# A decoder trunk on one core: the last norm on VectorE alone, modulation matmuls in quarters to four output rows, state-space parameters through GpSimd's queue, and the Toeplitz block shifted by TensorE

## The chip, the core and the metric

One core of a Trainium2 chip runs the whole kernel as one program. The metric is the time of one execution on the device in microseconds (us), as the median of several runs. The core's engines are TensorE (PE; its weight loads stand as PEld), VectorE (DVE), ScalarE (ACT), GpSimd (POOL) and SyncE (SP), which only issues transfers. Transfers can be issued by SyncE's queue and by GpSimd's.

## The reference, cut to what matters

```python
c_act = jax.nn.silu(c)
mod = c_act @ w_ada + b_ada                       # 6 vectors of 1024
sh1, sc1, g1, sh2, sc2, g2 = split(mod, 6)
h = rmsnorm(x, norm1_gain) * (1 + sc1) + sh1      # x: 1024 x 1024
proj = h @ w_in                                   # columns of four head groups
o_sb = stick_breaking_attention(...)              # 4 heads of 64, blocks of 128
o_sw = sliding_window_attention(..., rel_bias, sinks)
o_fx = forgetting_attention(...)
o_ssm = s5_ssm(u, lam, log_dt, b, c, d_skip, w_glu, b_glu)   # 16 groups of 16 channels
x = x + g1 * (groupnorm(concat(o_sb, o_sw, o_fx, o_ssm)) @ w_out)
h = rmsnorm(x, norm2_gain) * (1 + sc2) + sh2
x = x + g2 * (square(relu(h @ w_mlp_in)) @ w_mlp_out)         # 1024 -> 4096 -> 1024
return rmsnorm(x, final_gain)
```

All of it is in 32-bit floats. The large products keep that precision by splitting each operand into a high and a low part and summing three matmuls.

## The kernel before, in words

The program `tile_trunk` is written as one long sequence; a planner of the framework fixes, when the program is built, the order of the instructions on every engine, from estimates of their lengths and dependences. So an edit at one place can move instructions elsewhere on the same engine. Tiles of a pool with one tag share a fixed number of buffers.

The stages, by the trace of the kernel before:

- 0 to 57 us: x and the shift and scale quarters of `w_ada` are loaded. `shift_scale` (L210) multiplies the activated condition, widened to 32 columns, with them (L217), four matmuls of 128 columns per weight tile, to the output rows 0, 32, 64 and 96 upwards. `norm` scales the rows; `modulate` (L196) makes, for each of eight column blocks and two halves of the rows, a block of h with shift and scale in 32 bits (L199, VectorE), its rounded high part from the same source (L200, ScalarE) and the low part as the difference (L201; VectorE, for odd blocks of the second half GpSimd).
- 57 to 120 us: the projections of the stick-breaking heads (`mm3`, L253 to L255); beside them `ssm_prep` (L347) with many small VectorE instructions. There `cmul` makes complex products of six instructions each (L441 to L446): the powers `er`, `ei` and the products `qr`, `qi` on GpSimd. The parameters of the state-space head are loaded by SyncE (L331 to L340). The convolution block `kt` of 128 x 256 is written to device memory (`TD`) in eight copies shifted by 16 rows each, with zeros above (L541 and the line behind it). `window_bias` (L555) makes the bias of the sliding window.
- 115 to 350 us: stick-breaking attention by `sb_row`: scores (L639, L653), log-sigmoid and exponent on ScalarE, the mask product, the scan and the weighting on VectorE (L660, L662, L665), exponent (L666), transposes (L700) and mixing (L705). In between the other projections run, and `ada_rest` (L293), a generator that a row of attention advances three steps at a time: a step loads a weight tile of 128 x 1024 for one of four modulation vectors (L303) and multiplies it with the activated condition (L307).
- 350 to 600 us: `ssm_main`, forgetting and sliding-window attention (L733), out-projection.
- 600 to 664 us: the second norm and modulation by the same `modulate`, for `half0` and its fellows.
- 664 to 950 and 955 to 1262 us: the two products of the MLP.
- the end: `finish(t)` (L1378) for each of eight row tiles, after the tile's last sums: squares on ScalarE (L1385), a root by an estimate and one correction step (`rsqrt_mean`, L83 to L92), and the scaling by root and gain. Odd tiles (`FD_DVE`) do that with one VectorE instruction per half (L1390), even ones with ScalarE (L1393) and GpSimd (L1394).

Of the kernel before, what the change touches and what calls it, by code (L numbers as in the profile page):

```python
# [33 lines left out]
def tile_trunk(ctx: ExitStack, tc: tile.TileContext, a: dict, out: bass.AP):  # L34
# [69 lines left out]
    FD_DVE, EL = (1, 3, 5, 7), 2  # L104
# [142 lines left out]
    for f in range(KT):  # L247
        modulate(early, turn(ps1, "z", x1, f), f, h1s, h1b, hT[1][0][:, f], hT[1][1][:, f], G if f % 2 else V)
# [100 lines left out]
    def ssm_prep(pp):  # L349
# [130 lines left out]
        SY.dma_start(out=ED[0], in_=er)  # L480
        SY.dma_start(out=ED[1], in_=ei)
# [11 lines left out]
        cmul(qr, qi, pw(pr, 0), pw(pi, 0), mh(bbr), mh(bbi), sp4(d1), sp4(d2), G)  # L493
# [20 lines left out]
        SY.dma_start(out=WD[0], in_=wr.rearrange("p t k h -> p t (k h)"))  # L514
        SY.dma_start(out=WD[1], in_=wi.rearrange("p t k h -> p t (k h)"))
# [18 lines left out]
        z2 = pp.tile([P, 256], F32, name="z2")  # L534
        V.memset(z2, 0.0)
        for i in range(8):
            n = 16 * (7 - i)
            gh = lambda y: y.rearrange("q (g h) -> q g h", h=16)
            SY.dma_start(out=TD[n:P, :, i, :], in_=gh(kt[0:P - n, :]))
            if n:  # L540
                SY.dma_start(out=TD[0:n, :, i, :], in_=gh(z2[0:n, :]))  # L541
        for r, q in enumerate((qr, qi)):
            for b in range(2):
                ps = psm.tile([P, 4, P], F32, tag="ss", name="ps")
                for t in range(4):
# [3 lines left out]
                SY.dma_start(out=VTD[r][:, 4 * b:4 * b + 4, :], in_=vt)  # L549
# [6 lines left out]
    def window_bias(pp):  # L556
# [9 lines left out]
        SY.dma_start(out=RD, in_=rr[0:4, 0:384])  # L566
# [5 lines left out]
        SY.dma_start(out=Bf.rearrange("p (h c) -> p h c", h=4),  # L572
# [805 lines left out]
    def finish(t):  # L1378

        y = acc[t]  # L1380
        ss = sx.tile([P, 2], F32, tag="n3ss", bufs=2, name="ss")
        halves = [slice(n * 512, n * 512 + 512) for n in range(2)]
        for n, cs in enumerate(halves):
            sq = sx.tile([P, 512], F32, tag="sq", bufs=2, name="sq")
            A.activation(sq, y[:, cs], AF.Square, accum_out=ss[:, n:n + 1])  # L1385
        V.tensor_tensor(ss[:, 0:1], ss[:, 0:1], ss[:, 1:2], op=ALU.add)
        r = rsqrt_mean(sx, ss[:, 0:1], D, 1, "n3")
        for n, cs in enumerate(halves):
            if t in FD_DVE:
                V.scalar_tensor_tensor(out=y[:, cs], in0=y[:, cs], scalar=r[:, 0:1], in1=fg[:, cs],  # L1390
                                       op0=ALU.mult, op1=ALU.mult)
            else:
                A.activation(y[:, cs], y[:, cs], AF.Copy, scale=r[:, 0:1])  # L1393
                G.tensor_tensor(y[:, cs], y[:, cs], fg[:, cs], op=ALU.mult)  # L1394
            SY.dma_start(out=out[t * P:(t + 1) * P, cs], in_=y[:, cs])
# [95 lines left out]
```

## Time and profile before

| what | value |
|---|---|
| runs | 1277.53, 1278.24, 1279.88 us, median 1278.24 |
| the profiled execution, whole time | 1281.41 us |
| its span in the trace | 1279.3 us |
| mean granted TensorE clock | 0.976 of full speed |
| moved by transfers | 205.37 MB, 161 GB/s on average |

The span runs from the first to the last instruction of the trace; the profiled execution's own time is 2.1 us longer, and it is 3.2 us longer than the median of the runs. The page lists how long every engine was busy; windows show the same for a stretch of the span, with the clock that TensorE was granted in it (1.00 is 2.4 GHz, 0.5 is 1.2 GHz) and the share of the transfer engines. Waits and the chain name what ended an engine's idle time.

### The profile page before, as it was taken

The numbers are of one execution on the slowest core, as the hardware profiler recorded it, in microseconds if no ns is written. First come the engines' busy times: TensorE is split into PE (matmuls) and PEld (weight loads), VectorE is DVE, ScalarE is ACT, GpSimd is POOL, SyncE is SP. The second block draws the span as 40 slices with busy tenths as digits, with TensorE's granted clock in tenths as the row PEclk, the third lists the DMA queues.
The fourth block names the chain that finished last, engine by engine and source line by source line (L and its number), as shares of the span: only waits on it lengthen the run. The fifth ranks groups of instructions, "written<-read, shape, count | busy, mean of one in ns | idle before, by whom it ended". The sixth has DMA issues, their size and how long they took to land.

```text
span 1279.3 us, 18741 instructions
## 1 busy us (share of the span) xinstructions
PE 1214.4 (95%) x6461; PEld 945.6 (74%) x6461; DVE 955.3 (75%) x2100; ACT 562.4 (44%) x1205; POOL 125.3 (10%) x171
## 2 busy tenths in 40 slices
PE   5899899999999998999899999999989999999994
PEld 3578677665677776888668888888867888888883
DVE  4685977775465687888998677767666777788998
ACT  4433555762224557545563232333344543433425
POOL 1218100000020100000000000000031210100003
PEclk9999899999999898999989999999999999999997
DMA  8664376576654655202124553443578653643413
GB/s 297 201 198 146 139 195 212 175 221 185 215 175 153 238 152 175 88 26 83 67 66 166 172 167 131 155 154 130 170 250 315 213 168 108 182 127 91 138 48 132
DMA packets 139334, 205.37 MB, mean 161 GB/s; under 512 B 37057, under 2 KB 77912, under 8 KB 139240
## 3 DMA queue, kind: packets, MB, share of 16 engines
q1 hardware_dynamic: 129768, 170.62, 41.6%
q0 software_dynamic: 9472, 33.56, 8.4%
q8 instruction: 51, 0.84, 0.3%
q14 instruction: 43, 0.35, 0.1%
HBM read 144.59 MB, written 59.55 MB: 160 GB/s over the span
## 4 chain that ended last, share of the span: by engine, by line
PE 80%; DVE 8%; DMA 7%; ACT 2%; issue 2%; SPq 1%; DVEq 0%; ACTq 0%
PE x L255 9%; PE x L253 9%; PE x L254 8%; PE y L254 6%; PE y L255 6%; PE y L253 6%; PE ps L253 6%; PE ps L254 6%; PE ps L255 6%; PE pv L705 3%; PE tp L700 3%; PE z L639 3%; PE ps L307 2%; DMA wa<-in_w_ada_dram 2%; DMA kk<-kd 1%
## 5 line engine op out<-in xcount | busy, mean ns | idle before, releaser
L1091 ACT CAST hi<-s 128x512 fp32r<-128x512 f32 x124 | 75.9, 618 | 110.8 <-PE x L254 36.7
L1091 ACT CAST hi<-hid 128x512 fp32r<-128x512 f32 x101 | 62.2, 618 | 129.7 <-issue 58.1
L254 PE MATMUL x<-lo,hi 128*128 128x512 f32 x256 | 98.3, 389 | 0.3 <-DVE lo L1092 0.3
L253 PE MATMUL x<-hi 128*128 128x512 f32 x256 | 95.9, 390 | 2.4 <-ACT hi L1091 2.4
L255 PE MATMUL x<-hi,lo 128*128 128x512 f32 x256 | 97.8, 389 | 0.0
L1092 DVE TENSOR_TENSOR lo<-raw,hi 128x512 fp32r<-128x512 f32 x97 | 65.9, 686 | 40.8 <-PE x L255 21.6
L253 PE MATMUL ps<-hT_hi,wh 128*128 128x512 f32 x224 | 90.8, 417 | 4.9 <-DVE e L273 2.6
L255 PE MATMUL ps<-hT_hi,wl 128*128 128x512 f32 x224 | 91.5, 411 | 1.5 <-DVE wl L185 1.5
L1091 ACT CAST hi<-raw 128x512 fp32r<-128x512 f32 x97 | 59.1, 619 | 74.2 <-PE y L254 45.9
L254 PE MATMUL ps<-hT_lo,wh 128*128 128x512 f32 x224 | 91.2, 408 | 0.0
L1092 DVE TENSOR_TENSOR lo<-s,hi 128x512 fp32r<-128x512 f32 x124 | 84.2, 684 | 3.1 <-ACT hi L1091 2.1
L1092 DVE TENSOR_TENSOR lo<-hid,hi 128x512 fp32r<-128x512 f32 x101 | 69.1, 685 | 21.1 <-ACT hi L1091 19.0
L255 PE MATMUL y<-hi,lo 128*128 128x512 f32 x196 | 75.3, 389 | 0.0
L254 PE MATMUL y<-lo,hi 128*128 128x512 f32 x196 | 75.2, 389 | 0.0
L253 PE MATMUL y<-hi 128*128 128x512 f32 x196 | 73.6, 390 | 0.3 <-ACT hi L1091 0.3
L700 PE MATMUL tp<-ident,w 128*128 128x128 f32 x348 | 60.3, 288 | 5.7 <-ACT w L666 5.5
L703 DVE COPY wt<-tp 128x512 f32<-128x512 f32 (+1 forms) x68 | 42.8, 638 | 27.2 <-PE tp L700 25.7
L1273 POOL DMA_DIRECT2D raw<-in_w_mlp_out_dram x64 | 34.4, 540 | 258.6 <-DVE lo L1092 75.1
L1099 POOL DMA_DIRECT2D raw<-in_w_mlp_in_dram x16 | 14.4, 898 | 453.9 <-DVE lo L1092 384.9
L253 PEld LDWEIGHTS x<-hi 128*128 128x128 f32 x256 | 48.0, 188 | 13.1 <-ACT hi L1091 3.2
L639 PE MATMUL z<-kk,s 128*128 128x256 f32 (+2 forms) x192 | 55.2, 382 | 2.5 <-DMA kk<-kd 2.5
L700 PEld LDWEIGHTS tp<-ident,w 128*128 128x128 f32 x348 | 40.0, 144 | 23.8 <-issue 11.2
(416 smaller groups left out, 3261.2 us busy)
## 6 DMA issues: line engine op xcount, KB each, us to landing
hid<-hh SPq DMA_DIRECT2D x101, 256.0 KB
wa<-in_w_ada_dram SPq DMA_DIRECT2D x32, 512.0 KB
raw<-in_w_mlp_in_dram POOLq DMA_DIRECT2D x16, 1024.0 KB, 7.0
raw<-in_w_mlp_out_dram POOLq DMA_DIRECT2D x64, 256.0 KB, 4.5
hh<-x SPq DMA_DIRECT2D x60, 256.0 KB
hh<-h SPq DMA_DIRECT2D x49, 256.0 KB
s<-qd SPq DMA_DIRECT2D x96, 128.0 KB
wa<-in_w_ada_dram SPq DMA_DIRECT2D x32, 256.0 KB
```

The costliest lines, as they stand in the source:

```text
L253: T.matmul(ps, wh, xh, start=first, skip_group_check=more, stop=False)
L254: T.matmul(ps, wh, xl, start=False, skip_group_check=more, stop=False)
L255: T.matmul(ps, wl, xh, start=False, skip_group_check=more, stop=last)
L307: T.matmul(ps[32 * r:32 * r + 1, :], cact[:, k:k + 1], w[:, n * 512:(n + 1) * 512], start=k == 0, stop=k == KT - 1)
L639: T.matmul(z[:, 0:n], q[r][:, qs], kk[:, 0:n], start=r == 0, stop=stop and r == 1)
L700: T.transpose(tp[:, b, :], w, ident)
L703: (A.copy if copies[0] % 2 and both else V.tensor_copy)(wt[:, 0:len(part)], tp[:, 0:len(part)])
L705: T.matmul(pv[x * HD:x * HD + HD, i % 2, :], v[:, kb, hs[x]], wt[:, b, :], start=n == 0, stop=n == len(ws[0]) - 1)
L1091: A.copy(shape(hi), src)
L1092: V.tensor_tensor(shape(lo), src, shape(hi), op=ALU.subtract)
L1099: G.dma_start(out=raws[i].rearrange("p (k c) -> p k c", k=KT), in_=w1[:, i * 256:i * 256 + 256].rearrange("(k p) c -> p k c", p=P))
L1273: load = G.dma_start(out=raw2[i, kind], in_=w2[(2 * i + x) * P:(2 * i + x + 1) * P, n * 512:n * 512 + 512])
```

## The change

The change does six things.

1. `finish` takes the tiles in groups (0,1), (2,3), (4,5), 6 and 7. All halves are scaled by the VectorE instruction (now L1399); ScalarE's scaling and GpSimd's product go. The small steps of the root are done once for a group.
2. `modulate` makes the 32-bit block on ScalarE, its high part as a copy of that block on ScalarE, and all low parts on VectorE.
3. `ada_rest` multiplies each weight tile in four matmuls of 256 columns, to the output rows 0, 32, 64 and 96, where there were two of 512 to two of these rows. The rows' bias loads and stores are cut accordingly: eight stores instead of four for a pair of vectors.
4. The parameter loads, the stores of `ED`, `WD`, `TD`, `VTD` and the transfers of the window bias and the sinks are issued by GpSimd instead of SyncE.
5. The complex product for `qr` and `qi` is VectorE's instead of GpSimd's.
6. The eight shifted copies of `kt` are made by eight matmuls with a window of a widened identity, copied out of PSUM by ScalarE into two tiles, and stored by two transfers in place of fifteen.

```diff
-    FD_DVE, EL = (1, 3, 5, 7), 2
+    EL = 2
...
-        V.tensor_scalar(h32, src, sc[:, f:f + 1], bi[:, f:f + 1], op0=ALU.mult, op1=ALU.add)
-        A.activation(dst_hi, src, AF.Identity, bias=bi[:, f:f + 1], scale=sc[:, f:f + 1])
+        A.activation(h32, src, AF.Identity, bias=bi[:, f:f + 1], scale=sc[:, f:f + 1])
+        A.copy(dst_hi, h32)
         eng.tensor_tensor(dst_lo, h32, dst_hi, op=ALU.subtract)
...
-        modulate(early, turn(ps1, "z", x1, f), f, h1s, h1b, hT[1][0][:, f], hT[1][1][:, f], G if f % 2 else V)
+        modulate(early, turn(ps1, "z", x1, f), f, h1s, h1b, hT[1][0][:, f], hT[1][1][:, f], V)
...
         for k in range(KT):
             for i, j in enumerate(js):
-                for c in range(0, D, wide):
-                    w = tile()
-                    SY.dma_start(out=w, in_=a["w_ada"][0, k * P:(k + 1) * P, j * D + c:j * D + c + wide])
-                    yield
-                    for n in range(wide // 512):
-                        r = 2 * i + c // 512 + n
-                        T.matmul(ps[32 * r:32 * r + 1, :], cact[:, k:k + 1], w[:, n * 512:(n + 1) * 512],
-                                 start=k == 0, stop=k == KT - 1)
+                w = tile()
+                SY.dma_start(out=w, in_=a["w_ada"][0, k * P:(k + 1) * P, j * D:j * D + D])
+                yield
+                for r in range(4):
+                    T.matmul(ps[32 * r:32 * r + 1, i * 256:i * 256 + 256], cact[:, k:k + 1], w[:, r * 256:r * 256 + 256],
+                             start=k == 0 and i == 0, skip_group_check=True, stop=k == KT - 1)
         for r in range(4):
             o = row[32 * r:32 * r + 1, :]
             V.tensor_tensor(o, ps[32 * r:32 * r + 1, :], o, op=ALU.add)
-            SY.dma_start(out=MD[js[r // 2]][:, r % 2 * 512:r % 2 * 512 + 512], in_=o)
+            for i, j in enumerate(js):
+                SY.dma_start(out=MD[j][:, r * 256:r * 256 + 256], in_=o[:, i * 256:i * 256 + 256])
...
-    SY.dma_start(out=ld, in_=a["log_dt"][0].rearrange("(t g) -> t g", g=2))
+    G.dma_start(out=ld, in_=a["log_dt"][0].rearrange("(t g) -> t g", g=2))
...
-        SY.dma_start(out=ED[0], in_=er)
+        G.dma_start(out=ED[0], in_=er)
...
-        cmul(qr, qi, pw(pr, 0), pw(pi, 0), mh(bbr), mh(bbi), sp4(d1), sp4(d2), G)
+        cmul(qr, qi, pw(pr, 0), pw(pi, 0), mh(bbr), mh(bbi), sp4(d1), sp4(d2))
...
-        z2 = pp.tile([P, 256], F32, name="z2")
-        V.memset(z2, 0.0)
-        for i in range(8):
-            n = 16 * (7 - i)
-            gh = lambda y: y.rearrange("q (g h) -> q g h", h=16)
-            SY.dma_start(out=TD[n:P, :, i, :], in_=gh(kt[0:P - n, :]))
-            if n:
-                SY.dma_start(out=TD[0:n, :, i, :], in_=gh(z2[0:n, :]))
+        shift = pp.tile([P, 2 * P], F32, name="shift")
+        V.memset(shift[:, 0:P], 0.0)
+        V.tensor_copy(shift[:, P:2 * P], ident)
+        td = [big("dt0"), big("dt1")]
+        for i in range(0, 8, 2):
+            ps = psm.tile([P, 2, 256], F32, tag="ss", name="ps")
+            for x in range(2):
+                n = 16 * (7 - i - x)
+                T.matmul(ps[:, x, :], shift[:, P - n:2 * P - n], kt, start=True, stop=True)
+            for b in range(2):
+                A.copy(td[b].rearrange("q g (i h) -> q i g h", h=16)[:, i:i + 2],
+                       ps.rearrange("q i (b g h) -> q b i g h", b=2, h=16)[:, b])
+        for b in range(2):
+            G.dma_start(out=TD[:, 8 * b:8 * b + 8].rearrange("q g i h -> q g (i h)"), in_=td[b])
...
-    def finish(t):
+    def finish(ts):
...
+        n = len(ts)
+        ss = sx.tile([P, 2, 2], F32, tag="n3ss", bufs=2, name="ss")
+        for x, t in enumerate(ts):
+            for h in range(2):
+                sq = sx.tile([P, 512], F32, tag="sq", bufs=2, name="sq")
+                A.activation(sq, acc[t][:, h * 512:h * 512 + 512], AF.Square, accum_out=ss[:, h, x:x + 1])
+        V.tensor_tensor(ss[:, 0, 0:n], ss[:, 0, 0:n], ss[:, 1, 0:n], op=ALU.add)
+        r = rsqrt_mean(sx, ss[:, 0, 0:n], D, n, f"n3{n}")
+        for x, t in enumerate(ts):
+            for h in range(2):
+                cs = slice(h * 512, h * 512 + 512)
+                y = acc[t][:, cs]
+                V.scalar_tensor_tensor(out=y, in0=y, scalar=r[:, x:x + 1], in1=fg[:, cs], op0=ALU.mult, op1=ALU.mult)
+                SY.dma_start(out=out[t * P:(t + 1) * P, cs], in_=y)
...
-        finish(t)
+        if t % 2 or t == 6:
+            finish({1: (0, 1), 3: (2, 3), 5: (4, 5)}.get(t, (t,)))
```

Three places of the order on the engines show what moves. Line numbers of the changed kernel are up to 7 higher.

On TensorE, in the attention rows: the modulation matmuls (`wa`, `cact`) among the projections (`wh`, `wl`, `hT`) and the attention. Before:

```order
L253 MATMUL ps<-wh,hT_hi 128x260
L700 MATMUL tp<-ident,w 128x128
L705 MATMUL pv<-wt,v_sb 64x128 x3
L307 MATMUL ps<-wa,cact 1x512 x2
L705 MATMUL pv<-wt,v_sb 64x128 x3
L700 MATMUL tp<-ident,w 128x128 x7
L254 MATMUL ps<-wl,hT_hi 128x260
```

Now:

```order
L253 MATMUL ps<-wh,hT_hi 128x260
L307 MATMUL ps<-wa,cact 1x256 x4
L712 MATMUL pv<-wt,v_sb 64x128 x4
L307 MATMUL ps<-wa,cact 1x256 x4
L254 MATMUL ps<-wl,hT_hi 128x260
L646 MATMUL z<-kk,s_2529 128x512
L646 MATMUL z<-kk,s_2531 128x512
```

Each weight tile has four short matmuls in place of two, and two tiles stand closer to each other here.

On VectorE, at the first attention rows (`aa`, `w`: the scan and the weighting; `wh`, `wl`: splits of the projections' weights). Before:

```order
L185 TENSOR_TENSOR wl<-raw,wh 128x2x256
L184 CAST wh<-raw 128x2x256
L660 TENSOR_SCALAR aa<-w 128x384
L185 TENSOR_TENSOR wl<-raw,wh 128x2x256
L660 TENSOR_SCALAR aa<-w 128x512
L184 CAST wh<-raw 128x2x256
L662 SCALAR_TENSOR_TENSOR aa<-tt,aa 128x384
L185 TENSOR_TENSOR wl<-raw,wh 128x2x256
L665 TENSOR_TENSOR w<-w,aa 128x384
L662 SCALAR_TENSOR_TENSOR aa<-tt,aa 128x512
L665 TENSOR_TENSOR w<-w,aa 128x512
```

Now, where L667, L669 and L672 are the former L660, L662 and L665, and L442 to L445 the products for `qr` and `qi`:

```order
L184 CAST wh<-raw 128x2x256
L667 TENSOR_SCALAR aa<-w 128x384
L185 TENSOR_TENSOR wl<-raw,wh 128x2x256
L667 TENSOR_SCALAR aa<-w 128x512
L442 TENSOR_TENSOR d_1503<-pr,bbr 128x1024
L443 TENSOR_TENSOR d_1504<-pi,bbi 128x1024
L669 SCALAR_TENSOR_TENSOR aa<-tt,aa 128x384
L444 TENSOR_TENSOR qr<-d_1503,d_1504 128x1024
L672 TENSOR_TENSOR w<-w,aa 128x384
L669 SCALAR_TENSOR_TENSOR aa<-tt,aa 128x512
L667 TENSOR_SCALAR aa<-w 128x384
L445 TENSOR_TENSOR d_1503<-pr,bbi 128x1024
```

The last weight splits stand ahead of the first scan now, and the products of 128 x 1024 among the first rows.

On VectorE, at the end (`acc_9866` is row tile 7 before, `acc_9948` tile 7 now; the numbers below count the tiles down). Before:

```order
L1390 SCALAR_TENSOR_TENSOR acc_9864<-acc_9864,n3r,fg 128x512 x2
L1386 TENSOR_TENSOR ss<-ss 128x1
L89 TENSOR_TENSOR n3t<-n3r 128x1
L86 TENSOR_SCALAR n3v<-ss 128x1
L90 TENSOR_TENSOR n3t<-n3t,n3v 128x1
L91 TENSOR_SCALAR n3t<-n3t 128x1
L92 TENSOR_TENSOR n3r<-n3r,n3t 128x1
L89 TENSOR_TENSOR n3t<-n3r 128x1
L90 TENSOR_TENSOR n3t<-n3t,n3v 128x1
L91 TENSOR_SCALAR n3t<-n3t 128x1
L92 TENSOR_TENSOR n3r<-n3r,n3t 128x1
L1390 SCALAR_TENSOR_TENSOR acc_9866<-acc_9866,n3r,fg 128x512 x2
```

Now:

```order
L86 TENSOR_SCALAR n31v<-ss 128x1
L92 TENSOR_TENSOR n32r<-n32r,n32t 128x2
L1399 SCALAR_TENSOR_TENSOR acc_9945<-acc_9945,n32r,fg 128x512 x2
L1399 SCALAR_TENSOR_TENSOR acc_9946<-acc_9946,n32r,fg 128x512 x2
L1393 TENSOR_TENSOR ss<-ss 128x1
L89 TENSOR_TENSOR n31t<-n31r 128x1
L86 TENSOR_SCALAR n31v<-ss 128x1
L90 TENSOR_TENSOR n31t<-n31t,n31v 128x1
L91 TENSOR_SCALAR n31t<-n31t 128x1
L92 TENSOR_TENSOR n31r<-n31r,n31t 128x1
L89 TENSOR_TENSOR n31t<-n31r 128x1
L1399 SCALAR_TENSOR_TENSOR acc_9947<-acc_9947,n31r,fg 128x512 x2
```

Behind the last row follow three small steps and the two instructions of tile 7. The products of tiles 4, 5, 6 and 7 are all VectorE's, where before only those of 5 and 7 stood there.

## Rows read from the trace of the kernel before

**Rows 1.** The page: span, and busy time, share and instructions of each engine.

```profile
span 1279.3 us, 18741 instructions
...
PE 1214.4 (95%) x6461; PEld 945.6 (74%) x6461; DVE 955.3 (75%) x2100; ACT 562.4 (44%) x1205; POOL 125.3 (10%) x171
```

**Rows 2.** Windows: length, busy us (instructions) by engine, PEclk, DMA share, GB/s.

```profile
115.30:134.04 18.74, 15.88 (x78) 12.48 (x77) 18.07 (x9) 6.87 (x15) 17.61 (x9) 1.00 0.32 99
125.00:150.00 25.00, 17.29 (x86) 13.71 (x85) 24.79 (x27) 11.04 (x20) 8.14 (x4) 0.86 0.34 115
150.00:400.00 250.00, 249.24 (x1589) 172.49 (x1589) 168.88 (x367) 121.95 (x270) 6.54 (x5) 0.99 0.61 187
500.00:525.00 25.00, 18.99 (x119) 15.77 (x118) 14.11 (x57) 13.72 (x43) 0.00 (x0) 0.80 0.49 161
600.00:665.00 65.00, 58.22 (x265) 45.00 (x265) 61.72 (x126) 37.42 (x72) 1.71 (x2) 0.95 0.14 49
629.00:665.00 36.00, 29.22 (x121) 21.06 (x119) 35.19 (x65) 22.28 (x37) 1.71 (x2) 0.91 0.10 30
```

**Rows 3.** Waits of PE: us in total, times, longest us.

```profile
PE tp L700 <- ACT w L666: 5.5, 1, 5.5
```

**Rows 4.** Instruction groups: count | busy us, mean ns of one | idle before.

```profile
L1233 DVE SCALAR_TENSOR_TENSOR h<-r 128x512 f32<-128x512 f32 x64 | 42.5, 685 | 5.8 <-ACT r L1232 5.7
...
L307 PE MATMUL ps<-wa,cact 128*1 128x512 f32 x128 | 32.8, 591 | 0.8 <-DMA wa<-in_w_ada_dram 0.8
```

**Rows 5.** Chain that ended last: start us, us, engine, line, pieces.

```profile
40.14 1.28 PE ps L217 x40
...
61.29 1.85 DMA dskip<-in_ssm_d_dram
...
190.85 0.86 PE ps L577 x2
...
239.77 0.96 PE ps L307 x4
...
500.49 8.10 DMA kk<-kd
```

**Rows 6.** Timeline of VectorE: start us, us, instruction, count [idle before <-releaser].

```profile
51.15 1.16 DVE L581 TENSOR_SCALAR nsink<-nsink 128x4 f32<-128x4 f32 x1 [4.01 <-DMA nsink<-in_sinks_dram]
...
130.99 3.13 DVE L662 TENSOR_TENSOR_SCAN aa<-tt,aa 128x384 f32<-128x384 f32 x1
...
137.46 0.96 DVE L662 TENSOR_TENSOR_SCAN aa<-tt,aa 128x384 f32<-128x384 f32 x1
...
143.26 1.22 DVE L509 TENSOR_TENSOR d<-pi,ct 128x1024 f32<-128x1024 f32 x1
```

**Rows 7.** Timeline of SyncE's queue, 58 to 115 us.

```profile
58.77 0.30 SPq L331 DMA_DIRECT2D ld<-in_log_dt_dram  x1
...
114.82 0.33 SPq L480 DMA_DIRECT2D ed<-er  x1
```

**Rows 8.** Durations by line, ns min/median/max, first and last start: L199, L1099.

```profile
L199 DVE TENSOR_SCALAR h<-ps,h1s,h1b x8: 790/800/810, 59.6 to 75.1; 128x512 f32<-128x512 f32 x8
L199 DVE TENSOR_SCALAR h<-ps,h2s,h2b x8: 802/803/811, 606.9 to 628.3; 128x512 f32<-128x512 f32 x8
...
L1099 POOL DMA_DIRECT2D raw<-in_w_mlp_in_dram x16: 882/884/1082, 497.9 to 896.2; - x16
```

**Rows 9.** Timelines of the tail: PE, then VectorE, then GpSimd.

```profile
1262.15 0.39 PE L255 MATMUL x<-hi,lo 128*128 128x512 f32 x1
...
1271.77 0.16 DVE L92 TENSOR_TENSOR n3r<-n3r,n3t 128x1 f32<-128x1 f32 x1
1271.96 3.50 DVE L1390 SCALAR_TENSOR_TENSOR acc<-acc,n3r,fg 128x512 f32<-128x512 f32 x2
...
1271.98 2.93 POOL L1394 TENSOR_TENSOR acc<-acc,fg 128x512 f32<-128x512 f32 x2 [2.10 <-ACT acc L1393]
```

More of the change, by code (lines that the diff above doesn't have):

```diff
@@ L334, in tile_trunk @@
     for t, nm in ((br, "ssm_b_re"), (bi, "ssm_b_im")):
-        SY.dma_start(out=t, in_=a[nm][0].rearrange("(t g) p h -> (g p) t h", g=2))
+        G.dma_start(out=t, in_=a[nm][0].rearrange("(t g) p h -> (g p) t h", g=2))
     cl = prep.tile([P, 2, 2, HD], F32, name="cl")
     for r, nm in enumerate(("ssm_c_re", "ssm_c_im")):
-        SY.dma_start(out=cl[:, r], in_=a[nm][0].rearrange("(b g) h p -> (g h) b p", b=2))
+        G.dma_start(out=cl[:, r], in_=a[nm][0].rearrange("(b g) h p -> (g h) b p", b=2))
     dskip = prep.tile([16, 256], F32, name="dskip")
-    SY.dma_start(out=dskip, in_=a["ssm_d"].rearrange("o g h -> o (g h)").to_broadcast([16, 256]))
+    G.dma_start(out=dskip, in_=a["ssm_d"].rearrange("o g h -> o (g h)").to_broadcast([16, 256]))
     mag8 = const.tile([P, 8], F32, name="mag8")
@@ L479, in ssm_prep @@
             k *= 2
-        SY.dma_start(out=ED[0], in_=er)
-        SY.dma_start(out=ED[1], in_=ei)
+        G.dma_start(out=ED[0], in_=er)
+        G.dma_start(out=ED[1], in_=ei)
         ct = pp.tile([P, 4, 8, 16], F32, name="ct")
@@ L513, in ssm_prep @@
         V.tensor_tensor(wi, e1, e2, op=ADD)
-        SY.dma_start(out=WD[0], in_=wr.rearrange("p t k h -> p t (k h)"))
-        SY.dma_start(out=WD[1], in_=wi.rearrange("p t k h -> p t (k h)"))
+        G.dma_start(out=WD[0], in_=wr.rearrange("p t k h -> p t (k h)"))
+        G.dma_start(out=WD[1], in_=wi.rearrange("p t k h -> p t (k h)"))
         cb = pp.tile([P, 2, 8, 32], F32, tag="o", bufs=2, name="cb")
@@ L548, in ssm_prep @@
                 A.copy(vt, ps)
-                SY.dma_start(out=VTD[r][:, 4 * b:4 * b + 4, :], in_=vt)
+                G.dma_start(out=VTD[r][:, 4 * b:4 * b + 4, :], in_=vt)
     ssm_prep(prep)
@@ L559, in window_bias @@
         V.memset(rel[32:33, :], NEG)
-        SY.dma_start(out=rel[0:32, :], in_=a["rel_bias"])
+        G.dma_start(out=rel[0:32, :], in_=a["rel_bias"])
         oh, rr = big("oh"), big("rr")
-        SY.dma_start(out=oh[0:33, 0:384], in_=a["onehot"])
+        G.dma_start(out=oh[0:33, 0:384], in_=a["onehot"])
         ps = psm.tile([P, 512], F32, tag="ss", bufs=1, name="ps")
@@ L565, in window_bias @@
         V.tensor_copy(rr[0:4, 0:384], ps[0:4, 0:384])
-        SY.dma_start(out=RD, in_=rr[0:4, 0:384])
+        G.dma_start(out=RD, in_=rr[0:4, 0:384])
         base = RD[:, :]
@@ L571, in window_bias @@
         Bf, B = big("Bf"), big("B")
-        SY.dma_start(out=Bf.rearrange("p (h c) -> p h c", h=4),
+        G.dma_start(out=Bf.rearrange("p (h c) -> p h c", h=4),
                      in_=bass.AP(tensor=base.tensor, offset=base.offset, ap=[[1, P], [384, 4], [1, 256]]))
@@ L578, in window_bias @@
             V.tensor_copy(B[:, cs], ps)
-        SY.dma_start(out=BD.rearrange("a p h c -> p a (h c)"), in_=B.rearrange("p (a c) -> p a c", a=2))
-        SY.dma_start(out=nsink, in_=a["sinks"].to_broadcast([P, 4]))
+        G.dma_start(out=BD.rearrange("a p h c -> p a (h c)"), in_=B.rearrange("p (a c) -> p a c", a=2))
+        G.dma_start(out=nsink, in_=a["sinks"].to_broadcast([P, 4]))
         V.tensor_scalar(nsink, nsink, -1.0, None, op0=ALU.mult)
@@ L923, in ada_all @@
         for js in ((2, 4), (3, 5)):
-            yield from ada_rest(js, D, lambda: ssm.tile([P, D], F32, tag="U", bufs=2, name="wa"),
+            yield from ada_rest(js, lambda: ssm.tile([P, D], F32, tag="U", bufs=2, name="wa"),
                                 ssm.tile([P, 512], F32, tag="s4", bufs=S4, name="row"))
@@ L1376, in gated @@
         V.tensor_tensor(acc[t][:, cs], acc[t][:, cs], rest_of[t][:, cs], op=ALU.add)
-    def finish(t):
[L1380 to L1395, printed above, removed]
+    def finish(ts):
[13 more added lines that the diff above has]
+                SY.dma_start(out=out[t * P:(t + 1) * P, cs], in_=y)
     last = load_raw(chunks[0], (0, 2, 1, 3)).ins
```

7 lines of the change are left out of this document (4 added, 3 removed).

## The prediction, made before the changed kernel had run

> **What bounds the kernel now.** The page comes first [rows 1]: TensorE is busy 95% of a span of 1279.3 us, VectorE 75%, ScalarE 44%, GpSimd 10%. So 65 us without TensorE work are all that waits can give; everything else must come out of TensorE's own work. The table of windows says where each holds [rows 2]. From 150 to 400 us TensorE is busy 249.24 of 250 us: there only fewer TensorE microseconds count. Around 125 to 150 it is busy 17.29 of 25 while VectorE is busy 24.79, and in 115.30 to 134.04 VectorE is at 18.07 of 18.74 in nine instructions, beside nine of GpSimd (17.61): VectorE sets the pace. From 600 to 665 VectorE is again at 61.72 of 65, and from 629 on TensorE idles 6.8 us. In the list of waits of TensorE single gaps are few; the largest behind ScalarE is one of 5.5 us at L700 [rows 3].
>
> The profiled execution took 1281.41 us, the median of the runs is 1278.24, 3.2 less. The sum is made against 1281.41, and 3.2 taken off at the end.
>
> **The modulation matmuls (L307).** Now 32 weight tiles take two matmuls of 512 columns each, 128 records of 591 ns [rows 4]; the two of a tile go to two output rows and overlap, so a tile costs 0.96 us [rows 5]. Afterwards a tile has four matmuls of 256 columns to rows 0, 32, 64 and 96. The nearest row with four output groups at once is L217: 40 records, that is five tiles of four matmuls of 128 columns, two records each, in 1.28 us, 0.256 a tile [rows 5]. Twice the columns: 0.51. Saved: 0.45 x 32 = **14.4 us**, all in the window with no TensorE idle. Bounds: 0, if the four don't overlap beyond two, and 15.4 (half of 0.96 each). L217 puts 32 rows in a group where these put one; the overlap is of groups, so I take 14.4.
>
> **The Toeplitz block.** Fifteen stores of small pieces leave SyncE's queue; eight matmuls of 256 columns come. L577, 512 columns of the same type, takes 0.86 [rows 5]; 0.43 x 8 = **3.4 us** more on TensorE, whose queue is full. Bounds 0 (all in a gap) and 6.9 (each as dear as L577). The eight copies are ScalarE's, which is busy 121.95 of the 250 us: costed at nothing; without that cover some 0.6 us each.
>
> **First attention rows.** The six products of 128x1024 leave GpSimd for VectorE. Each costs 1.22 there (L509 [rows 6]), 7.3 in all. But GpSimd's stand beside VectorE's work, which is slowed: the 128x384 scan takes 3.13 at 130.99 and 0.96 at 137.46, when GpSimd is done [rows 6]. By that ratio of 3.3 the nine instructions of the 18.07 us would take 5.5, a relief of 12.5; less 7.3 is **5.2 us** earlier. The order agrees: the weight splits now stand ahead of the first attention rows. TensorE has that much to give: 7.7 us idle in 125 to 150 and a clock of 0.86. Bounds: 2 (only the idle inside 115.30 to 134.04, 2.9, and part of it) and 13 (the relief, with the products behind). To the better side speaks that SyncE's queue stood until 114.82 for a store that waits for GpSimd [rows 7], weight loads behind it; that store is on GpSimd's queue now.
>
> **half0 and the second modulation.** Eight L199 of 803 ns [rows 8], 6.4 us, leave VectorE, which is 95% busy there, and ScalarE (37.42 of 65) gets eight copies. Each low part now follows two ScalarE steps instead of one, so I take 1.4 back: **5 us**. Bounds 0 (the chain, not the load, is the limit) and 10 (6.8 idle plus 0.09 of 36 us of clock). The first modulation has the same edit and four low parts more on VectorE: 8 x 0.8 us away [rows 8], four subtractions on. Costed at nothing, since VectorE only loses work there and TensorE is still fed by arriving weights; bare of that cover, it is within 3 us either way.
>
> **The last norm.** TensorE's last matmul ends at 1262.54, VectorE's last pair of products at 1275.46, 12.9 us later [rows 9]. Those pairs take 3.5 us beside GpSimd's products of 2.93; the same operation alone takes 685 ns (L1233 [rows 4]), some 1.2 a pair. Along the new order of VectorE, with two pairs of tiles still to be multiplied when TensorE ends: tile 7's last half added at +1.8, four products at 0.6 to +4.2, six small steps, 0.2 from one to the next, to +5.4, tile 6's pair to +6.6, and behind two or three steps that are left tile 7's pair to +8.3. So **4.6 us**. Bounds 0 and 6.9 (both late pairs gone from the path).
>
> **The queues.** SyncE loses some thirty issues; six parameter loads and later stores are GpSimd's, idle by then. The nearest issues on GpSimd take 882 to 1082 ns (L1099 [rows 8]). They begin near 58.77, as SyncE's did [rows 7]. The last one, dskip, landed in 1.85 [rows 5]; its reader now stands behind six low parts. Eight L199 spread over 59.6 to 75.1 [rows 8], so it is needed near 69, and six issues may take 1.4 us each: nothing lost. The sink's load moves to the start of GpSimd's queue, and VectorE's wait of 4.01 for it [rows 6] goes; TensorE has work through it: nothing gained. By the Trainium skill, SBUF — State Buffer, "Who interferes with whom", GpSimd can't write a transfer's descriptors while VectorE copies or scales in a two-port mode; the issues above ran beside subtractions for the most part and show no such spread, so the trace neither bears this out nor excludes it. Its figure under "SBUF: two separate sides", some 3.1 us for a transfer that alone takes 0.62, would put about 10 us on the sum, an estimate from that page.
>
> **Loads before forgetting attention.** At 500.49 TensorE waits for keys that took 8.10 us [rows 5]; the new order puts such loads elsewhere among GpSimd's and SyncE's transfers. I take 0, between a loss and a gain of 5.
>
> Sum: -14.4 + 3.4 - 5.2 - 5 - 4.6 = -25.8, so 1255.6 for a profiled execution, **1252.4** for the median.
>
> **Rivals.**
> *B. The saving at L307 doesn't arrive*, as only two of the four run at a time or VectorE and ScalarE set the pace of these rows: 1252.4 + 14.4 = 1266.8. For it: each of the four now needs its own weights, and no row shows one-row outputs four at a time. Against: L217's 0.256, and VectorE's 168.88 of 250.
> *C. The parameters come late through GpSimd's queue.* If an issue is held up to three times L1099's row, 2.7 us, six cost 6 x (2.7 - 1.4) = 8 us, with the low parts and so TensorE behind them: 1260. It decides from 1.4 us an issue on. Against: 1.08 is the longest seen.
> *D. Slower: new gaps in the attention stages.* With 11 us less of TensorE's work in 150 to 400 (14.4 less 3.4), a row waits for scan, exponent and transposes, as once at L700 (5.5 us [rows 3]). Priced by the window 500 to 525, a gap costs 6.0 idle and, at a granted clock of 0.80, 5 more: 11. From the third on (25.8 / 11 = 2.3) the change is slower; with three, 1285. Against: VectorE has 80 us free in 150 to 400, ScalarE 128.
> *E. Better:* the gap at 500 closes too, 11 us: 1241. For it: SyncE's queue is shorter; against: that wait is for keys stored and reloaded, which nothing here shortens.
>
> **Numbers.** The forecast 0.62, B 0.13, C 0.10, E 0.07, D 0.08. The range 1241 to 1268 takes in B, C and E and leaves out D and parts that miss together. About 0.2%, 2.6 us, is what a measurement of this kernel can tell from no change: faster 0.91, same 0.02, slower 0.07.
>
> **What would show it.** Right: the four L307 records of a tile begin together and a tile takes near 0.5 us; the scan of the first row under 1.5 us; GpSimd without products after 120 us; TensorE idle after 629 down by some 4 us; VectorE's last pair 8 us after the last matmul. B would show L307 tiles at 0.96 or idle before L639 and L700; C a VectorE wait for ld or dskip between 60 and 75; D new TensorE gaps over 4 us and a clock near 0.8 behind them. Wrong altogether is the prediction if the windows from 150 to 400 are no shorter in sum.

## The result and the profile after

The changed kernel takes 1255.72 us (median of five runs, 1254.36 to 1258.59) against 1277.53 for the kernel before: ratio 0.9829, 95% interval 0.981 to 0.9848, 21.8 us faster. The forecast was 1252.4. The profiled execution took 1254.91 us (its span is 1253.2), 26.5 less than the profiled execution before and 0.7 less than the sum's 1255.6; the 3.2 us taken off for the median were not there this time, since the profiled execution of before lay above its median and that of after lies below.

The page of the changed kernel, which answers to [rows 1]:

```profile
span 1253.2 us, 19015 instructions
...
PE 1201.2 (96%) x6605; PEld 946.0 (75%) x6605; DVE 932.0 (74%) x2077; ACT 567.8 (45%) x1223; POOL 107.3 (9%) x175
```

TensorE is busy 13.2 us less and idle 12.9 us less (65 to 52). Not all of the 13.2 is work that went: the mean granted clock rose from 0.976 to 0.986, and a matmul of 128x512 at L253 that takes 0.39 us at a clock of 1.00 takes 0.79 at 133.31 in the changed kernel, where the clock is 0.5. Where the time went, the windows tell. Of the kernel before, columns as in [rows 2], where the window from 629 to 665 stands:

```profile
100.00:150.00 50.00, 42.29 (x266) 36.93 (x265) 34.48 (x36) 19.24 (x39) 31.24 (x39) 0.93 0.39 126
400.00:550.00 150.00, 141.26 (x946) 109.35 (x945) 111.36 (x381) 84.24 (x228) 8.31 (x7) 0.93 0.52 164
425.00:450.00 25.00, 24.86 (x183) 18.80 (x183) 17.37 (x62) 15.35 (x33) 3.72 (x3) 0.86 0.84 308
...
600.00:629.00 29.00, 29.00 (x146) 23.95 (x147) 26.52 (x62) 15.14 (x35) 0.00 (x0) 1.00 0.19 73
```

Of the changed kernel, the same stages; the last two are 23 us earlier, as the stage itself is:

```profile
100.00:150.00 50.00, 46.80 (x272) 40.24 (x272) 33.31 (x42) 22.52 (x46) 17.15 (x30) 0.90 0.39 126
150.00:400.00 250.00, 245.67 (x1781) 180.52 (x1780) 171.03 (x385) 121.02 (x279) 12.78 (x16) 0.99 0.62 194
400.00:550.00 150.00, 149.36 (x1002) 116.60 (x1003) 125.26 (x404) 91.88 (x244) 9.04 (x7) 0.99 0.50 158
577.00:606.00 29.00, 29.00 (x151) 24.30 (x149) 21.54 (x55) 19.28 (x43) 0.00 (x0) 1.00 0.19 73
606.00:642.50 36.50, 29.44 (x122) 21.16 (x120) 34.95 (x65) 21.89 (x40) 1.23 (x2) 0.91 0.09 29
```

Four things are to be seen. At 100 to 150 TensorE is busy 4.5 us more, at a clock of 0.90 instead of 0.93, which takes up to 1.5 us of that back (0.03 of 50). From 400 to 550 its idle time fell from 8.7 to 0.6 us and the share missing from the clock from 0.07 to 0.01 of 150 us, 10.5 to 1.5; the 9 us of clock are an upper estimate, as part of the low clock fell where TensorE idled (500 to 525 in [rows 2]). In the second norm and modulation (600 to 665 before) nothing changed: 65.0 us before, 65.5 after, with the same 7 us idle, although VectorE is busy 5.2 us less in it. And the window from 150 to 400, with 0.8 us of idle time before [rows 2], now has 4.3.

Two waits of TensorE for keys, which stood at 400 to 550 before, are not in its list of the changed kernel:

```profile
PE z L733 <- DMA kk<-kd: 5.8, 1, 5.8
...
PE z L639 <- DMA kk<-kd: 2.5, 1, 2.5
```

The groups of the modulation and Toeplitz matmuls after; columns as in [rows 4]:

```profile
L307 PE MATMUL ps<-wa,cact 128*1 128x256 f32 x256 | 19.4, 377 | 1.6 <-DMA wa<-in_w_ada_dram 1.6
...
L543 PE MATMUL ps<-kt,shift 128*128 128x256 f32 x16 | 4.2, 385 | 0.0
```

And of the chain (start, us, line, records):

```profile
154.80 0.86 PE ps L543 x4
...
284.40 0.97 PE ps L307 x16
```

Sixteen records of L307 are two weight tiles: 0.49 us each, where 0.51 was predicted. The group's busy time fell from 32.8 [rows 4] to 19.4 us. The Toeplitz matmuls take 0.43 each, as predicted.

VectorE at the first attention rows, after:

```profile
122.59 0.43 DVE L184 CAST wh<-raw 128x512 fp32r<-128x512 f32 x1 [1.73 <-DMA raw<-in_w_in_dram]
...
123.80 0.42 DVE L667 TENSOR_SCALAR aa<-w 128x512 f32<-128x512 f32 x1
124.14 1.22 DVE L442 TENSOR_TENSOR d<-pr,bbr 128x1024 f32<-128x1024 f32 x1
...
126.41 0.95 DVE L669 TENSOR_TENSOR_SCAN aa<-tt,aa 128x384 f32<-128x384 f32 x1
127.28 1.20 DVE L444 TENSOR_TENSOR qr<-d,d 128x1024 f32<-128x1024 f32 x1
```

The scan takes 0.95 from the start (3.13 in [rows 6]), the products 1.2 each. GpSimd's queue, where the parameters are loaded:

```profile
59.81 0.53 POOL L332 DMA_DIRECT2D ld<-in_log_dt_dram  x1 [5.41 <-ACT h L199]
60.33 0.97 POOL L336 DMA_DIRECT2D br<-in_ssm_b_re_dram  x1
...
63.63 0.53 POOL L341 DMA_DIRECT2D dskip<-in_ssm_d_dram  x1
```

VectorE, where the first and the last of them are read:

```profile
61.53 0.21 DVE L401 COPY ldx<-ld 8x128 f32<-8x128 f32 x1
...
69.59 0.41 DVE L532 TENSOR_TENSOR dskip<-dskip,ident 16x256 f32<-16x256 f32 x1
```

The six issues take 0.53 to 0.97 us. Neither the row of `ld` nor that of `dskip` shows idle time ahead of it. TensorE's last matmul after:

```profile
1240.04 0.39 PE L255 MATMUL x<-hi,lo 128*128 128x512 f32 x1
```

VectorE's last products:

```profile
1242.92 2.74 DVE L1399 SCALAR_TENSOR_TENSOR acc<-acc,n32r,fg 128x512 f32<-128x512 f32 x4
...
1246.50 1.41 DVE L1399 SCALAR_TENSOR_TENSOR acc<-acc,n31r,fg 128x512 f32<-128x512 f32 x2
...
1248.39 1.41 DVE L1399 SCALAR_TENSOR_TENSOR acc<-acc,n31r,fg 128x512 f32<-128x512 f32 x2
```

The last matmul ends at 1240.43, the last product at 1249.80: 9.4 us behind, not 8.3, against 12.9 before.

### The profile page after: what moved, and what is told of

It reads as the page before. It is cut to its first block, busy times and chain, and to the rows that moved or that the text cites. A ratio compares the mean times of both kernels' runs of the same rounds, so it can differ in the third digit from the quotient of the medians.

```text
span 1253.2 us, 19015 instructions
## 1 busy us (share of the span) xinstructions
PE 1201.2 (96%) x6605; PEld 946.0 (75%) x6605; DVE 932.0 (74%) x2077; ACT 567.8 (45%) x1223; POOL 107.3 (9%) x175
## 4 chain that ended last, share of the span: by engine, by line
PE 83%; DVE 6%; DMA 5%; issue 3%; ACT 3%; SPq 1%; POOL 0%; DVEq 0%; POOLq 0%; ACTq 0%
PE x L255 9%; PE x L254 9%; PE x L253 9%; PE y L254 7%; PE y L255 7%; PE y L253 7%; PE ps L253 7%; PE ps L254 6%; PE ps L255 6%; PE pv L712 3%; PE tp L707 3%; PE z L646 2%; DMA wa<-in_w_ada_dram 1%; PE ps L307 1%; DMA hid<-hh 1%
## 5 line engine op out<-in xcount | busy, mean ns | idle before, releaser
L253 PE MATMUL x<-hi 128*128 128x512 f32 x256 | 96.0, 390 | 2.4 <-ACT hi L1098 2.4
L1099 DVE TENSOR_TENSOR lo<-raw,hi 128x512 fp32r<-128x512 f32 x97 | 65.7, 684 | 41.9 <-PE x L255 21.7
L253 PE MATMUL ps<-hT_hi,wh 128*128 128x512 f32 x224 | 90.5, 414 | 6.5 <-DVE e L273 4.1
L1099 DVE TENSOR_TENSOR lo<-s,hi 128x512 fp32r<-128x512 f32 x124 | 83.9, 683 | 3.4 <-ACT hi L1098 2.6
L1099 DVE TENSOR_TENSOR lo<-hid,hi 128x512 fp32r<-128x512 f32 x101 | 68.9, 683 | 21.7 <-ACT hi L1098 19.6
L253 PE MATMUL y<-hi 128*128 128x512 f32 x196 | 73.7, 390 | 0.8 <-ACT hi L1098 0.8
L253 PEld LDWEIGHTS x<-hi 128*128 128x128 f32 x256 | 48.0, 188 | 13.2 <-ACT hi L1098 3.2
L254 PEld LDWEIGHTS x<-lo,hi 128*128 128x128 f32 x256 | 48.1, 188 | 10.6 <-DVE lo L1099 0.7
L253 PEld LDWEIGHTS ps<-hT_hi,wh 128*128 128x128 f32 x224 | 42.8, 194 | 17.5 <-DVE e L273 5.0
```

Source lines behind the costliest of these rows:

```text
L253: T.matmul(ps, wh, xh, start=first, skip_group_check=more, stop=False)
L254: T.matmul(ps, wh, xl, start=False, skip_group_check=more, stop=False)
L1099: V.tensor_tensor(shape(lo), src, shape(hi), op=ALU.subtract)
```

## The experiments

Every kernel was timed beside the kernel before. The ratios are to the kernel before; us are medians.

| kernel | us | ratio, 95% interval | against the changed kernel (1255.72, 0.9829) |
|---|---|---|---|
| no_quarters | 1269.37 | 0.9935 (0.9914 to 0.9957) | +13.7 |
| no_finish | 1259.36 | 0.9866 (0.9842 to 0.989) | +3.6 |
| mod2_V | 1257.63 | 0.984 (0.9815 to 0.9864) | +1.9 |
| no_mod | 1276.24 | 0.9988 (0.9969 to 1.0007) | +20.5 |
| no_mod_flip | 1265.26 | 0.9892 (0.986 to 0.9923) | +9.5 |
| no_cmul | 1276.57 | 1.0005 (0.999 to 1.002) | +20.9 |
| no_cmul_flip | 1283.14 | 1.0032 (1.0014 to 1.0051) | +27.4 |
| p_rr | 1256.64 | 0.9845 (0.9817 to 0.9873) | +0.9 |
| p_flip | 1264.62 | 0.99 (0.9876 to 0.9923) | +8.9 |
| q_clean | 1253.6 | 0.9812 (0.9783 to 0.9842) | -2.1 |
| no_queues | 1250.72 | 0.9788 (0.9764 to 0.9812) | -5.0 |
| no_toep | 1259.6 | 0.9845 (0.9812 to 0.9879) | +3.9 |

The medians of the kernel before differed by up to 2.5 us between the series, so differences of less than 3 us are read from the ratios only.

### Each part undone

**The modulation matmuls.**

```diff
-                for r in range(4):
-                    T.matmul(ps[32 * r:32 * r + 1, i * 256:i * 256 + 256], cact[:, k:k + 1], w[:, r * 256:r * 256 + 256],
+                    for n in range(wide // 512):
+                        r = 2 * i + c // 512 + n
+                        T.matmul(ps[32 * r:32 * r + 1, :], cact[:, k:k + 1], w[:, n * 512:(n + 1) * 512],
```

> The changed kernel with the modulation matmuls as before (two of 512 columns per weight tile). The sum's term: 0.96 instead of about 0.49 us per weight tile, 32 tiles, all on a full TensorE, so some 14 us slower than the changed kernel (1255.7): 1270. Rival, the attention rows' VectorE and ScalarE set the pace there: within 3 us of the changed kernel, with more TensorE idle before L646 and L707 in the changed one.

It was 13.7 us slower. The group of this kernel:

```profile
L307 PE MATMUL ps<-wa,cact 128*1 128x512 f32 x128 | 31.8, 591 | 0.3 <-DMA wa<-in_w_ada_dram 0.3
```

Its busy time is 31.8 against 19.4, 12.4 us. The term of the sum holds, and TensorE, not VectorE, limited these rows: rival B falls. The 13.7 were measured in one order of the instructions alone, so the busy time is the firmer of the two numbers.

**The last norm.**

```diff
-                V.scalar_tensor_tensor(out=y, in0=y, scalar=r[:, x:x + 1], in1=fg[:, cs], op0=ALU.mult, op1=ALU.mult)
+                A.activation(y[:, cs], y[:, cs], AF.Copy, scale=r[:, 0:1])
+                G.tensor_tensor(y[:, cs], y[:, cs], fg[:, cs], op=ALU.mult)
```

> The changed kernel with the last norm as before (even tiles by ScalarE and GpSimd). From the two traces, the last VectorE pair ends 12.9 us behind the last matmul before and 9.4 now: 3.5 us slower than the changed kernel, 1259. Rival, the end of the output stores sets the end: no change.

3.6 us slower (4.7 by the ratios). TensorE's order in this kernel is that of the changed one, so this price is clean. TensorE's last matmul in it:

```profile
1239.22 0.39 PE L255 MATMUL x<-hi,lo 128*128 128x512 f32 x1
```

VectorE's last products:

```profile
1249.02 3.50 DVE L1397 SCALAR_TENSOR_TENSOR acc<-acc,n3r,fg 128x512 f32<-128x512 f32 x2
```

GpSimd's last products, beside them:

```profile
1249.04 2.93 POOL L1401 TENSOR_TENSOR acc<-acc,fg 128x512 f32<-128x512 f32 x2 [2.10 <-ACT acc L1400]
```

The last product ends 12.9 us behind the last matmul again. GpSimd's help cost more than it gave: four halves took the two engines 3.5 us together, and VectorE alone takes 2.74 for four (the row at 1242.92).

**The second modulation.**

```diff
-            modulate(op, turn(ps2, "t", xn, f), f, h2s, h2b, hi, lo, V)
+            modulate(op, turn(ps2, "t", xn, f), f, h2s, h2b, hi, lo, None)
```

where `None` puts the 32-bit block on VectorE and its high part, from PSUM, on ScalarE, as before.

> The changed kernel with the 32-bit block of the second modulation alone on VectorE again; the order of the work ahead of it stays row by row. The prediction's term: 5 us slower, 1261. Rival, TensorE was full while these eight instructions ran and the idle behind is a chain: within 1.5 us of the changed kernel, so that no_mod's 20 us come from the first modulation and what is behind it.

The ratio moved by 0.0011 within intervals of 0.0025 on either side. The stage in this kernel:

```profile
582.00:647.50 65.50, 57.67 (x272) 44.99 (x271) 62.02 (x128) 37.80 (x73) 1.76 (x2) 0.97 0.13 49
```

VectorE is busy 62.02 us of these 65.5 again, 5.5 more than the two windows of the changed kernel together (56.49), and the stage is no longer: from the last matmul of the out-projection to TensorE's last matmul it is 642.0 us in the kernel before, 642.2 in the changed kernel and 640.8 in this one. The prediction's 5 us for half0 fall.

**Both modulations, and the products.** The first of these two kernels also gives the low parts of odd blocks in the second half back to GpSimd.

```diff
-        A.activation(h32, src, AF.Identity, bias=bi[:, f:f + 1], scale=sc[:, f:f + 1])
-        A.copy(dst_hi, h32)
+        V.tensor_scalar(h32, src, sc[:, f:f + 1], bi[:, f:f + 1], op0=ALU.mult, op1=ALU.add)
+        A.activation(dst_hi, src, AF.Identity, bias=bi[:, f:f + 1], scale=sc[:, f:f + 1])
```

> The changed kernel with the modulation block on VectorE again (both norms). The sum's term: 5 us slower, 1261, from VectorE's load at 600 to 665. Rival read from the changed trace: the eight L199 stood at 607 to 628, where TensorE was full, and the idle behind it is a chain: no change, within 2 us.

```diff
-        cmul(qr, qi, pw(pr, 0), pw(pi, 0), mh(bbr), mh(bbi), sp4(d1), sp4(d2))
+        cmul(qr, qi, pw(pr, 0), pw(pi, 0), mh(bbr), mh(bbi), sp4(d1), sp4(d2), G)
```

> The changed kernel with the product for qr and qi on GpSimd again. The sum's term: 5 us slower, 1261, the scan of the first attention row near 3 us again. Rival: only the queues matter there (weight loads stuck behind the store of ed): within 1 us of the changed kernel although VectorE is slowed.

Both missed both theories: each alone undoes nearly all of the gain, 20.5 and 20.9 us. The scan of the first attention row, expected near 3 us in no_cmul, takes 0.94, as it stands behind GpSimd's last product there (133.46):

```profile
133.66 0.94 DVE L669 TENSOR_TENSOR_SCAN aa<-tt,aa 128x384 f32<-128x384 f32 x1
```

With no_quarters and no_finish the prices add up to 59 us where the whole change brings 22. Parts with prices of their own that add up can't do that. Two explanations were left: the order that the planner comes to, which differs in more than a thousand rows of TensorE alone in either kernel, or a dependence between the parts.

### Order or price

Two edits that cost next to nothing rewrite the order.

```diff
-        V.tensor_copy(rr[0:4, 0:384], ps[0:4, 0:384])
+        A.copy(rr[0:4, 0:384], ps[0:4, 0:384])
```

> The changed kernel with one copy of 4 partitions x 384 (rr, near 191 us, some 0.4 us) on ScalarE instead of VectorE: nothing in it costs or saves, but the planner writes TensorE's and VectorE's order anew from there to about 580 us. If each part has its own price: within 1 us of the changed kernel. If the order alone moves gaps and clock: several us, up to 10 or 20, slower (or faster), with other gaps and low-clock stretches between 200 and 580.

```diff
-            V.tensor_copy(B[:, cs], ps)
+            A.copy(B[:, cs], ps)
```

> The changed kernel with the two copies of the window bias (B, near 207 us, 0.6 us each) on ScalarE instead of VectorE; as p_rr, a second new order from there on. Own prices: within 1 us of the changed kernel. Order: several us, not the same as p_rr.

One is the same within its interval, the other 8.9 us slower (0.7% by the ratios). So a new order alone is worth up to 9 us in these two. The same flip was then put on the two kernels that were in doubt; each has the edit of no_mod or no_cmul and that of p_flip, and no other.

> no_mod with the two copies of the window bias on ScalarE, which rewrites the order from near 200 us on. If the first modulation on VectorE has a price of 20 us of its own: again 1276 (or 1285 with what the flip cost on the changed kernel). If most of the 20 was the order that the planner came to: another time, 4 to 15 us faster, with the gaps behind 340 us gone or elsewhere.

> no_cmul with the two copies of the window bias on ScalarE. If the products on GpSimd cost 21 us of their own: again 1276 or more. If their own price is the 5 us of the first rows and the rest is order: another time, between 1261 and 1272, with the gap of 8 us near 130 still there.

With the flip, the modulation on VectorE costs nothing beyond the intervals: 1265.26 against p_flip's 1264.62 (ratios 0.9892 and 0.99). So its 20.5 us are no price of the part; what is left for them is the order, which in that kernel is worth 20 us and not 9. The windows of no_mod from 200 to 550 us:

```profile
200.00:343.00 143.00, 135.13 (x1018) 94.64 (x1016) 92.11 (x196) 71.77 (x167) 1.03 (x2) 0.95 0.67 215
343.00:550.00 207.00, 200.02 (x1357) 155.98 (x1354) 146.31 (x484) 103.47 (x267) 14.55 (x12) 0.94 0.50 158
```

and of no_mod_flip:

```profile
200.00:343.00 143.00, 138.57 (x1074) 97.33 (x1074) 96.63 (x209) 74.25 (x173) 0.72 (x1) 1.00 0.70 221
343.00:550.00 207.00, 202.17 (x1401) 157.59 (x1400) 157.88 (x505) 110.64 (x285) 14.54 (x12) 1.00 0.48 155
```

In the first, TensorE idles 5.6 us more and has a clock of 0.95 and 0.94, which is up to 7 and 12 us; neither stretch holds an instruction of `modulate`.

The products are the other case. With the flip they cost 18.5 us (1283.14 against 1264.62; 17 by the ratios), without it 20.9 (22). That is a price of the part, and a larger one than the prediction's 5. Waits of TensorE in no_cmul, which stand in no_cmul_flip as 8.7 (four waits, the longest 5.8), 4.6 and 1.2 us:

```profile
PE tp L707 <- ACT w L673: 8.0, 1, 8.0
...
PE ps L584 <- DMA Bf<-rd: 4.7, 1, 4.7
PE ps L253 <- DVE fpre L787: 3.2, 1, 3.2
```

In the changed kernel only the second of them is there:

```profile
PE ps L584 <- DMA Bf<-rd: 0.5, 1, 0.5
```

Windows of no_cmul and then of the changed kernel, whose row for 100 to 150 stands above:

```profile
100.00:150.00 50.00, 41.71 (x247) 35.97 (x245) 31.37 (x29) 19.45 (x40) 31.39 (x39) 0.90 0.34 111
200.00:250.00 50.00, 41.93 (x307) 31.87 (x306) 36.09 (x70) 30.76 (x72) 2.56 (x4) 0.90 0.48 156
```

```profile
200.00:250.00 50.00, 47.65 (x418) 37.39 (x418) 39.96 (x79) 34.81 (x83) 1.50 (x2) 1.00 0.65 202
```

At 100 to 150, 5.1 us of TensorE are lost at the same clock (46.80 against 41.71 busy), which is the predicted term. At 200 to 250 come 5.7 us idle and up to 5 us of clock (0.90 of 50), which are not in it. The two kernels with the flip show the same: 46.92 and 41.77 us busy in the first window, 47.78 and 40.42 in the second, where the clock is 1.00 and 0.86. The two longest waits at 200 to 250 are those for `Bf` and for `fpre` of VectorE. GpSimd's queue shows where the first comes from. Of no_cmul:

```profile
130.79 2.67 POOL L447 TENSOR_TENSOR qi<-d,d 128x1024 f32<-128x1024 f32 x1
153.88 0.58 POOL L515 DMA_DIRECT2D wd<-e_re  x1 [20.43 <-DVE e_re L511]
...
182.87 1.05 POOL L548 DMA_DIRECT2D td<-dt  x2 [18.59 <-ACT dt L545]
...
214.28 0.78 POOL L579 DMA_DIRECT2D Bf<-rd  x1 [4.29 <-DMA rd<-rr]
```

and of the changed kernel:

```profile
144.52 0.53 POOL L515 DMA_DIRECT2D wd<-e_re  x1 [26.32 <-DVE e_re L511]
...
172.43 1.05 POOL L548 DMA_DIRECT2D td<-dt  x2 [18.56 <-ACT dt L545]
...
200.53 0.78 POOL L579 DMA_DIRECT2D Bf<-rd  x1 [2.42 <-DMA rd<-rr]
```

The stores of WD and TD and the load of `Bf` come 9.4, 10.4 and 13.8 us later. GpSimd is idle ahead of each of them; each waits for what VectorE, ScalarE or a transfer has to finish first. The blocks behind them, the Toeplitz matmuls, the transposed products, the window bias and the modulation, take turns in one PSUM bank (the tag `ss`), so the first modulation matmul is later too, at 243 against 226 us. That the bank passes the delay on is read from the code and these rows; no run gave the blocks a bank each. The start of the modulation matmuls alone doesn't make the price: in no_toep below, without the Toeplitz matmuls in this chain, they start at 207.7, and the kernel is no faster.

### Queue and Toeplitz

```diff
-    G.dma_start(out=ld, in_=a["log_dt"][0].rearrange("(t g) -> t g", g=2))
+    SY.dma_start(out=ld, in_=a["log_dt"][0].rearrange("(t g) -> t g", g=2))
```

and so on for the other transfers that each expectation names.

> The changed kernel with the parameter loads and later stores on SyncE's queue again, all else as changed. The prediction gave this part nothing: within 2 us of the changed kernel. Rival E, the keys' loads at 404 and 500 came sooner because SyncE's queue is short: gaps before L646 and L740 of 2 to 6 us back, 10 us slower.

> The changed kernel with the six parameter loads, the sinks, the first bias loads and the stores of WD, TD and VTD on SyncE's queue again, and only ED, RD, Bf and BD left on GpSimd's: TensorE's order stays (12 rows differ), so this prices the queue without a new order. If GpSimd's queue itself costs: 3 to 5 us faster than the changed kernel, as no_queues was. If no_queues was faster by its order: within 2 us of the changed kernel.

no_queues has the lowest median of all kernels here, 5 us below the changed one (the intervals of the two ratios just touch), and missed both expectations. It shows no wait of TensorE for `kk<-kd` either, with all 22 issues back on SyncE. q_clean, with 17 of those 22 issues on SyncE and TensorE's order kept, is 2.1 us faster by the medians and the same within the intervals. So these 17 issues through GpSimd cost 2 us by the medians and some 7 at most by the intervals. Whether the rest of no_queues comes from the stores of `er`, `ei` and the bias transfers or from its order stays open.

```diff
-            G.dma_start(out=TD[:, 8 * b:8 * b + 8].rearrange("q g i h -> q g (i h)"), in_=td[b])
+            SY.dma_start(out=TD[n:P, :, i, :], in_=gh(kt[0:P - n, :]))
```

(the eight matmuls and copies go, the fifteen pieces return)

> The changed kernel with the Toeplitz block stored in fifteen pieces by SyncE again. The sum's term: 3.4 us faster, 1252. Rival: the pieces fill SyncE's queue ahead of weight loads and cost more than the matmuls: slower. Order can add 9 us either way, as p_flip showed, so only TensorE's time for L543 (16 records) is read as the term itself.

3.9 us slower by the medians and 2 by the ratios, less than an order can do. That shifting by TensorE gains is not shown; that it costs 8 x 0.43 us of TensorE is.

## Why the prediction was right, and where it was not

The time lies in the range and near the forecast, but that it came so near is in part luck. Two terms of the sum were wrong in opposite directions, and the sum has no term for the order that the planner comes to, which moved 9 us in p_flip and 20 in no_mod. No run separates the whole change from its order.

- **The modulation matmuls** (14.4): right. 0.49 us a tile against 0.51, 12.4 us of busy time and 13.7 of time by the experiment. The row with four output groups was the right neighbour, although it feeds 32 rows of each.
- **Toeplitz** (3.4): right for TensorE; its net effect is open.
- **First attention rows** (5.2): the place and the size were right: TensorE is busy 4.5 us more at 100 to 150, and 5.1 are lost there without the edit. The ratio that gave the size was not (last section). And the step stopped at 150 us: products on GpSimd cost the changed kernel 17 to 22 us in all, most of it later. Why so much less shows against the kernel before, which has them there too, is not shown; from the code, its Toeplitz block does not stand in the chain through the PSUM bank.
- **half0** (5): failed. The prediction took VectorE's 95% and TensorE's idle from one window of 65 us. Split at 629, the window shows that TensorE was full (29.00 of 29) while all eight L199 ran, and that the idle came behind them, where none was left. VectorE lost the 5 us of work, and nothing waited for it. The sign that was named for this term, some 4 us less idle time of TensorE behind 629, did not come: 6.8 us before, 7.1 after.
- **The last norm** (4.6): 3.5. The operation was priced by L1233's 685 ns, a form without a factor per row, and a pair at 1.2, where a pair of L1233 takes 1.28 in the trace before; with a factor per row it takes 746, and a pair 1.41. That makes 0.8 of the 1.1 us too little. The four products began 2.5 us behind the last matmul instead of 1.8, another 0.7, and the small steps took 0.4 less than was counted.
- **The queues** (0): right; six issues at 0.53 to 0.97 us against the 1.4 that they could take, and no wait for `ld` or `dskip`. Rival C falls. The rule of the Trainium skill on descriptors (SBUF — State Buffer, "Who interferes with whom") was hardly put to the test by these six: beside them VectorE ran subtractions for the most part. One later issue fits it: the store at L516 takes 1.16 us in no_cmul, from 163.11 to 164.27, with a scaling and a cast of VectorE beside it until 164.15, and 0.53 in the changed kernel, where no such instruction runs beside more than its start.
- **Loads before forgetting attention** (0, between -5 and 5): mis-sized. The two waits for `kk<-kd` (2.5 and 5.8 us before) are no longer in TensorE's list, and most of the low clock at 400 to 550 is gone: idle time fell by 8.1 us and clock by up to 9, together up to 17, where rival E had 11 for the gap at 500. Of the 10.5 that the clock cost before, some 3.5 (0.86 of 25 at 425 to 450) follow no such wait. Which edit did it stays open: rival E's reason, the shorter queue of SyncE, is not it, for no_queues has the long queue and no such wait. Not all of it is a gain of the edits: in the order of p_flip TensorE idles 4.5 us at 400 to 550, no_mod shows that an order can take as much back, and 3.6 us of new idle time at 150 to 400 did take some.
- **Rival D**, new gaps in attention: not in the changed kernel, but in no_mod and no_cmul, where the change less one part is no faster than the kernel before. A chance of 0.08 looks low for what one order decides.

## What to carry to other kernels

Before a relief of one engine is counted, cut the window where the relieved instructions end: idle time of the bound engine behind them is not theirs to give. Where a planner writes the order anew for every edit, undoing one part measures the part plus a new order; one or two edits that cost nothing give a first idea of how large that is (here 1 and 9 us, and yet 20 in no_mod), and the time that one undone part adds is its price only if it is there in two orders or the order stayed. Here that holds for the products, for the last norm and, at nothing, for the modulations; the modulation matmuls rest on their busy time, and the Toeplitz block and the queues, beyond q_clean's bound, have no price yet. Work that two engines share can be dearer than the same work on one of them, when they run side by side: compare four halves in 3.5 us with four in 2.74.

## What the runs showed that was not expected

In these rows a VectorE instruction beside GpSimd's products takes about as long as one of them, whatever its own length. VectorE in no_cmul, and one of GpSimd's products beside it:

```profile
124.07 2.61 DVE L184 CAST wh<-raw 128x512 fp32r<-128x512 f32 x1
...
131.18 2.56 DVE L667 TENSOR_SCALAR aa<-w 128x512 f32<-128x512 f32 x1
```

```profile
123.68 2.72 POOL L444 TENSOR_TENSOR qr<-d,d 128x1024 f32<-128x1024 f32 x1
```

The cast takes 2.61 and the scaling 2.56 us; in the changed kernel the same two forms take 0.43 and 0.42, and GpSimd's six products take 2.06 to 2.72. So a factor, as the prediction's 3.3, is the wrong picture: one instruction is exchanged for one. The Trainium skill has it so: by SBUF — State Buffer, "Who interferes with whom", the port pair that the two engines share is held for a whole instruction, and these rows agree. That the factor gave about the right size for the first attention rows is luck: the nine instructions of the 18.07 us take 5.1 alone, by the rows of the same forms, where it gave 5.5.

VectorE's instruction with a factor per row takes 746 ns for 128x512 (L1399) where the form of L1233, with a constant factor, takes 685, and L273, with a constant factor and two different inputs, 682. The first stood in the trace before as well, as L1029's 744.
